# Layer 0's token mixing as three fp32r products of split operands in place of one float32 product

## Chip, cores and metric

The kernel runs on one core of a Trainium2 chip. The metric is the device time of one execution in microseconds (us). In the profile, PE is TensorE's matmul, PEld its weight load, DVE is VectorE, ACT is ScalarE, POOL is GpSimd and SP is SyncE, which issues most DMAs. A line such as L1054 is line 1054 of the kernel before.

## The reference

The program is a two-layer trunk over 256 latent and 256 context tokens of width 2048. Each layer projects the normalised tokens to nine groups of columns, which feed three branches (a: a gated MLP that mixes tokens, b: attention, c: a Fourier mixing), and then projects back. What matters here is branch a:

```python
def chunk_gmlp(u, v, g_sgu, w_s, b_s):
    bsz, t, _ = v.shape
    nc = t // CHUNK
    vn = rmsnorm(v, g_sgu).reshape(bsz, nc, CHUNK, A_HEADS, A_DIM)
    mixed = jnp.einsum('hpq,bcqhd->bcphd', w_s, vn) + b_s.T[None, None, :, :, None]
    return u * mixed.reshape(bsz, t, A_WIDTH)

y_a = chunk_gmlp(jax.nn.gelu(a_u), jax.nn.gelu(a_v), g_sgu, w_s, b_s) * jax.nn.silu(a_g)
```

For each of four heads, every chunk of 128 tokens is multiplied by a 128x128 matrix over its tokens. Layer 0 has four chunks (two latent, two context), layer 1 works on the two latent ones alone.

## The kernel before

Nearly all large products are made in the type fp32r, to which a float32 value is cast with some loss. Each operand is held as a high part (the value cast to fp32r) and a low part (the value minus the high part), and a product is the sum of three: high x high, high x low, low x high. The helper `mm3` (L591 to L594) issues these three matmuls into one accumulator. In layer 0 nearly all of PE's work is of this kind. Branch a's mixing is an exception: a plain float32 matmul, `PE.matmul(ps[...], vt[t][...], ws[:, h], ...)` at L1054.

Weights arrive by the class `Stream` in pieces of 128 x 1024. `load` asks for a piece by DMA into one of three `raw` buffers; `emitting` then casts it on ACT (L560, the high part `whi`) and subtracts on DVE (L562, the low part `wlo`). Pieces are used in a fixed order, and `fetch` emits them up to three pieces ahead of the one that PE uses. Layer 0's opening takes 14 pieces (for av, the columns of v, and for the first three column groups of u), then follow two pieces each for au3 (the last group of u) and for the four groups cx0 to cx3 of the Fourier branch, and so on.

PE's instructions run in the order in which they are written. That order interleaves the column groups (`tunit`, 16 steps k of one `mm3` each) with the pieces of other branches, which are generators that a small clock, `Later`, resumes: each `yield` names how many microseconds of PE work are to pass before the next step, and `tick` advances that clock. From the end of layer 0's opening on, DVE, ACT and SP are not ordered by hand: a scheduler places their instructions by priority, which is the order in which they were emitted, as their inputs become ready in its own reckoning. `low(n)` gives instructions a later priority. Their order on the chip is then fixed.

`branch_a` (L1038 to L1061) is the first such generator behind the opening. Its first step, emitted before au3's products, applies GELU to u (L1042) and to the four chunks `vt` of v (L1044), sums squares (L1046), forms the reciprocal root with POOL's power (L617 to L623), and scales each chunk in place on DVE (L1049). It then yields 11 us of PE work. Each later step is one head: the float32 products of its chunks (L1054), then DVE's scale and bias (L1056), and the product with u (L1060). `fourier_mats` (L1071) comes soon behind it, with `split_into` (L608), which casts on ACT (L609) and subtracts on DVE (L610). In the background `mod_dve` (L310) sums the modulation of later stages on DVE (L321, L323).

Buffers have names (tags), and a tile that is claimed under a tag waits for the release of the one before. `new_yo(k)` claims the output buffer of 16 column groups, two of them in each of `yy0` to `yy7`. At the opening the same tags hold the inputs x, and `yy2`, `yy3` a piece of weights. At L1002 to L1004, when the opening is through, all 16 are claimed. Entries 0 to 3 hold branch a's u (`ytmp`), 12 to 15 the Fourier outputs, 4 to 11 attention.

Of the kernel before, what the change touches and what calls it, by code (L numbers as in the profile page):

```python
# [7 lines left out]
F32 = mybir.dt.float32  # L8
F32R = mybir.dt.float32r
BF16 = mybir.dt.bfloat16  # L10
AF = mybir.ActivationFunctionType
ALU = mybir.AluOpType

P = 128
# [52 lines left out]
def trunk_kernel(ctx: ExitStack, tc: tile.TileContext, xT, xhalf, cT, wss, wsl, wmod, win, wout0, wout1, const, vec, rows,  # L67
                 wmat, bs, sink, out):
    nc = tc.nc
    V, A, G, PE, DMA = nc.vector, nc.scalar, nc.gpsimd, nc.tensor, nc.sync  # L70
# [6 lines left out]
    def sb(shape, dt, tag, bufs=1):  # L77
        cnt[0] += 1
        return pool.tile(shape, dt, tag=tag, bufs=bufs, name=f"{tag}_{cnt[0]}")

    def w2k(shape, dt=F32):
        return sb(shape, dt, "w2k", W2K)
# [5 lines left out]
    def ms_ps(name="ms"):  # L88
        cnt[0] += 1
        return psum.tile([P, 512], F32, tag="ms", bufs=2, name=f"ps_{name}_{cnt[0]}")  # L90
# [18 lines left out]
    def new_yo(j):  # L109
        if j % 2 == 0:  # L110
            t = sb([P, 2, T], F32, f"yy{j // 2}")
            yo[j], yo[j + 1] = t[:, 0], t[:, 1]
        return yo[j]
# [44 lines left out]
    def vc(l, name):  # L158
        o, w = VOFF[name]
        return vecs[:, l, o:o + w]  # L160
# [252 lines left out]
    LOWC = 60  # L413
    LOWP = 60, 0
    YT = 3.0
    GATES = {2: 0, 14: 1}, {14: 2}, {12: 3}, {}
    YG = 6.5
    MODEND = 53.0, 45.0
# [172 lines left out]
    def mm3(ps, st, mv, start, stop):  # L591
        PE.matmul(ps, st[0], mv[0], start=start, stop=False)  # L592
        PE.matmul(ps, st[0], mv[1], start=False, stop=False)  # L593
        PE.matmul(ps, st[1], mv[0], start=False, stop=stop)  # L594

    def part(w, c):

        def of(t):
            if not isinstance(t, list):
                return t[:, c]  # L600
            n = t[0].shape[-1]
            return t[c.start // n][:, c.start % n:c.start % n + c.stop - c.start]

        return of(w[0]), of(w[1])
# [3 lines left out]
    def split_into(hi, lo, src):  # L608
        A.copy(hi, src)  # L609
        V.tensor_tensor(out=lo, in0=src, in1=hi.bitcast(F32), op=ALU.subtract)  # L610
        return hi, lo

    def split_of(src, tag):
        n = src.shape[-1]
        return split_into(sb([P, n], F32R, tag + "h"), sb([P, n], F32R, tag + "l"), src)


    def rstd_cols(sums, n, dim):
        t = sb([P, 4], F32, "rs_a", 2)
        V.tensor_scalar(out=t[:, :n], in0=sums, scalar1=1.0 / dim, scalar2=EPS, op0=ALU.mult, op1=ALU.add)  # L620
        r = sb([P, 4], F32, "rs_b", 2)
        G.tensor_tensor(out=r[:, :n], in0=t[:, :n], in1=mhalf[:, :n], op=ALU.pow)  # L622
        return r  # L623
# [28 lines left out]
    def h_of(l, k, sl):  # L652

        if l == 0:
            return hh[k][:, sl], hl[k][:, sl]
        s, a = sl.start // S, sl.start % S
        t, b = (hh, hl)[s][k], a + sl.stop - sl.start
        return t[:, a:b], t[:, S + a:S + b]
# [75 lines left out]
    def tunit(n, sl=None):  # L734

        sl = slice(0, n) if sl is None else sl
        ps = mm_ps("t")
        for k in range(KT):
            if k % 8 == 0:
                w = W.next()  # L740
            c = slice((k % 8) * P, (k % 8 + 1) * P)
            mm3(ps[:, sl], part(w, c), (hh[k][:, sl], hl[k][:, sl]), k == 0, k == KT - 1)
            later.tick(PASS * n)
        return ps
# [6 lines left out]
    def joined(ps):  # L751

        t = sb([P, S], F32, "join", 2)
        A.copy(t, ps[:, S:T])
        V.tensor_tensor(out=t, in0=t, in1=ps[:, 0:S], op=ALU.add)
        return t

    def tunit1(streams):

        pss = [mm_ps("t") for _ in streams]  # L760
        for k in range(KT):
            if k % 8 == 0:
                w = W.next()
            for s, ps in zip(streams, pss):
                mm2(ps, part(w, slice((k % 8) * P, (k % 8 + 1) * P)), (hh, hl)[s][k], k)
                later.tick(PASS * S)
        return [joined(ps) for ps in pss]
# [12 lines left out]
    def layer(l):  # L780
        last = l == 1
        n = S if last else T
        nt = n // P
# [217 lines left out]
            start_au(k0 + nk - 1)  # L1001
        if l == 0:  # L1002
            for k in range(KT):
                new_yo(k)  # L1004

            DMA.dma_start(cst[:, NFIRST - P:], const[:, NFIRST:NKEEP])
            with low(LOWC):
                for name in ("m0", "ct", "nst"):
                    o, w = COFF[name]
                    raw = w2k([P, w])  # L1010
                    DMA.dma_start(raw, const[:, o:o + w])
                    if w == P:
                        split[name] = sb([P, 2, P], BF16, f"{name}r")
                        raw0 = raw
                        A.copy(split[name][:, 0], raw)
                    else:
                        split[name] = split_of(raw, f"{name}r")

        ws = sb([P, 4, P], F32, "ws")
# [18 lines left out]
        def branch_a():  # L1038
            vt = [w2k([P, 512]) for _ in range(nt)]
            ss = sb([P, 4], F32, "ss")  # L1040
            for j in range(len(au)):
                A.activation(ytmp(j), joined(au[j]) if last else au[j], AF.Gelu_apprx_tanh)  # L1042
            for t in range(nt):
                A.activation(vt[t], av[t], AF.Gelu_apprx_tanh)  # L1044
            for t in range(nt):
                A.activation(av[t], vt[t], AF.Square, accum_out=ss[:, t:t + 1])  # L1046
            r = rstd_cols(ss[:, 0:nt], nt, 512)
            for t in range(nt):
                V.tensor_scalar(out=vt[t], in0=vt[t], scalar1=r[:, t:t + 1], scalar2=None, op0=ALU.mult)  # L1049
            yield 11.0 if l == 0 else 7.0  # L1050
            for h in range(4):
                ps = ms_ps("mix")
                for t in range(nt):
                    PE.matmul(ps[:, t * P:(t + 1) * P], vt[t][:, h * P:(h + 1) * P], ws[:, h], start=True, stop=True)  # L1054
                m = w2k([P, nt, P])
                V.scalar_tensor_tensor(out=m, in0=ps[:, 0:n].rearrange("p (t q) -> p t q", q=P),  # L1056
                                       scalar=vc(l, "gsgu")[:, h:h + 1],
                                       in1=bsb[:, h].unsqueeze(1).to_broadcast([P, nt, P]),
                                       op0=ALU.mult, op1=ALU.add)
                V.tensor_tensor(out=ytmp(h), in0=ytmp(h), in1=m.rearrange("p t q -> p (t q)"), op=ALU.mult)  # L1060
                yield (4.0 if h == 1 else 2.0) if l == 0 else (7.0 if h == 1 else 2.0)  # L1061


# [145 lines left out]
        if l == 0:  # L1209
            later.add(turn_mask(), 1.5)  # L1210
        later.add(branch_a())
        later.add(fourier_mats(), (3.0, 1.5)[l])
        later.tick(0.0)
        state["phase"] = f"au{l}"
        for h in range(len(au), 4):
            ps = tunit1([0])[0] if last else tunit(n)
# [3 lines left out]
        for g in range(4):  # L1220
            ps = tunit1([0])[0] if last else tunit(n)
# [3 lines left out]
        for h in range(4):  # L1225
            ps = tunit1([0])[0] if last else tunit(n)
            gate(h, ps)
        state["phase"] = f"cg{l}"
        for g in range(4):
            ps = tunit1([0])[0] if last else tunit(n)  # L1230
# [3 lines left out]
        r = sb([P, 4, S], F32, "mgl")  # L1234
# [9 lines left out]
        for k in range(KT):  # L1244
# [3 lines left out]
            for t in range(4):  # L1248
                hi, lo = h_of(l, k, slice(t * P, (t + 1) * P))
# [5 lines left out]
        for h in range(8):  # L1255
            ps = tunit1([0])[0] if last else tunit(n)
# [3 lines left out]
        for h in range(8):  # L1260
            ps = tunit1([0])[0] if last else tunit(n)
# [67 lines left out]
    def finish():  # L1329
# [3 lines left out]
        def turn():  # L1333

            for j, tag in enumerate(("vv", "mg", "mgl", "kt0 kt1")):
                tag = tag.split()
                tl = [sb([P, 2 // len(tag), 512], F32, t) for t in tag]
                for t in range(2):
                    x1[j, t] = tl[0][:, t] if len(tl) == 1 else tl[t][:, 0]
                    ps = ms_ps("x1")  # L1340
                    for i in range(4):
                        PE.transpose(ps[:, i * P:(i + 1) * P], yo[4 * j + i][:, t * P:(t + 1) * P], ident)
                    A.copy(x1[j, t], ps)
                    yield YT

        later.add(turn(), YT)
        state["phase"] = "out1"
# [49 lines left out]
        for c in range(4):  # L1397
# [3 lines left out]
            for k in range(KT + back):  # L1401
# [10 lines left out]
                later.tick(PASS * 1024)  # L1412
                if k in GATES[c]:
                    later.add(gate1(GATES[c][k]))
            evac(c, 1, pss[1])
# [92 lines left out]
    with tc.manual_schedule(engines={EN.PE}):  # L1508
# [11 lines left out]
        for i in range(KT):  # L1520
            h, j = i // 8, i % 8
            x = xx[2 * (j // 2) + h][:, j % 2 * 2:j % 2 * 2 + 2]
            q = w2k([P, 2, S])
# [9 lines left out]
            for a in range(2):  # L1533
                k = 2 * j + a
                PE.matmul(sq[32 * (k % 4):32 * (k % 4) + 32, h * S:(h + 1) * S], ones[:, 0:32], q[:, a],
                          start=k < 4, stop=k >= KT - 4, tile_position=(0, 32 * (k % 4)))
# [19 lines left out]
        ps = sums  # L1556
# [22 lines left out]
        for s in range(2):  # L1579
            scale_x(1, rb0, s, 2)  # L1580
        state["e0"] = e
        layer(0)
        state["acc"] = out_proj()
        layer(1)
        finish()

# [76 lines left out]
```

## Time and profile before

| what | value |
|---|---|
| median of three timed runs | 1116.06 us (1115.85 to 1116.09) |
| profiled execution, whole time | 1115.65 us |
| profiled execution, span | 1113.9 us |
| granted TensorE clock | 0.999 |
| ACT busy, share of the span | 49% |
| POOL busy, share of the span | 3% |
| mean DMA rate | 212 GB/s |

The span is the profiled part of an execution; the time around it belongs to start and end. Times in rows are microseconds from the start of the span. In a timeline, a row has the start, the length, the engine, the line, the operation, the output and inputs with shape, and the count of merged instructions; in brackets is how long the engine had been idle and what released it. Matmuls overlap in the pipeline, so their recorded lengths add up to more than the time they hold PE; the distance between starts is the better measure. In the answer for one line, three numbers with slashes are the shortest, median and longest duration in ns.

### The profile page before, as it was taken

What the parts mean: (1) busy time and instruction counts of PE and PEld (TensorE: products, weight loads), DVE (VectorE), ACT (ScalarE), POOL (GpSimd) and SP (SyncE); (2) the same over time, 40 slices, a digit from 0 to 9 for tenths busy, and PEclk for the clock granted to TensorE, in tenths of its full rate; (3) what the DMA queues carried; (4) which work ended last, traced back from release to release, by engine and by line L of the source; (5) the groups of instructions that cost most, each with busy time, mean ns of one, the idle gap of its engine ahead of it and who ended that gap; (6) DMA issues with size and microseconds to landing.
All of it is one profiled execution on the core that took longest, in us unless ns stands there. A gap on an engine that the chain in (4) does not pass through costs nothing. (4 is left out here: it accounts for less than half of the span.)

```text
span 1113.9 us, 17364 instructions
## 1 busy us (share of the span) xinstructions
PE 1104.0 (99%) x6450; PEld 926.4 (83%) x6453; DVE 926.4 (83%) x1616; ACT 550.7 (49%) x1049; POOL 33.4 (3%) x43
## 2 busy tenths in 40 slices
PE   8999999999999999999999999999999999999998
PEld 4777888888888888888888888988888888898886
DVE  3677599999988897988998989397889789878974
ACT  4454823322335667632533333256665379867542
POOL 1000000000000000000000000030500000000000
PEclk9999999999999999999999999999999999999999
DMA  9999655577665353465556665376956686556881
GB/s 376 413 414 410 226 191 169 189 226 215 201 190 174 109 161 114 141 196 184 169 190 209 210 218 177 112 184 202 229 172 206 223 288 199 160 175 205 302 265 75
DMA packets 75525, 235.89 MB, mean 212 GB/s; under 512 B 8480, under 2 KB 15024, under 8 KB 75440
## 3 DMA queue, kind: packets, MB, share of 16 engines
q1 hardware_dynamic: 71088, 230.31, 62.3%
q0 software_dynamic: 4064, 3.69, 2.2%
q8 instruction: 50, 0.82, 0.3%
q10 hardware_dynamic: 288, 0.79, 0.2%
q14 instruction: 35, 0.29, 0.1%
HBM read 232.65 MB, written 2.10 MB: 211 GB/s over the span
## 5 line engine op out<-in xcount | busy, mean ns | idle before, releaser
L560 ACT CAST whi<-raw 128x1024 fp32r<-128x1024 f32 (+1 forms) x210 | 216.6, 1035 | 302.3 <-PE ps_t L593 186.0
L592 PE MATMUL ps_t<-hh,whi 128*128 128x512 f32 (+1 forms) x752 | 290.9, 387 | 0.0
L594 PE MATMUL ps_t<-hh,wlo 128*128 128x512 f32 (+1 forms) x752 | 289.8, 385 | 0.0
L593 PE MATMUL ps_t<-hl,whi 128*128 128x512 f32 (+1 forms) x752 | 289.5, 385 | 0.0
L562 DVE TENSOR_TENSOR wlo<-raw,whi 128x1024 fp32r<-128x1024 f32 (+1 forms) x210 | 251.0, 1199 | 40.6 <-ACT whi L560 34.7
L323 DVE SCALAR_TENSOR_TENSOR macc<-mraw,cs,macc 128x512 f32<-128x512 f32 x360 | 251.5, 745 | 12.7 <-DMA mraw<-in_wmod_dram 12.1
L748 PE MATMUL ps_t<-hh,whi 128*128 128x512 f32 x512 | 181.2, 394 | 0.0
L594 PEld LDWEIGHTS ps_t<-hh,wlo 128*128 128x128 f32 x752 | 141.3, 188 | 28.7
L592 PEld LDWEIGHTS ps_t<-hh,whi 128*128 128x128 f32 x752 | 141.4, 188 | 26.5
L593 PEld LDWEIGHTS ps_t<-hl,whi 128*128 128x128 f32 x752 | 141.4, 188 | 26.4
L749 PE MATMUL ps_t<-hh,wlo 128*128 128x256 f32 x512 | 142.2, 278 | 0.0
L748 PEld LDWEIGHTS ps_t<-hh,whi 128*128 128x128 f32 x512 | 96.2, 188 | 19.3
L749 PEld LDWEIGHTS ps_t<-hh,wlo 128*128 128x128 f32 x512 | 96.2, 188 | 0.4
L592 PE MATMUL ps_y<-whi,hh 128*128 128x512 f32 x104 | 41.3, 397 | 0.0
L594 PE MATMUL ps_y<-whi,hh 128*128 128x512 f32 x104 | 40.6, 391 | 0.0
L593 PE MATMUL ps_y<-wlo,hh 128*128 128x512 f32 x104 | 40.6, 390 | 0.0
L609 ACT CAST w2k<-ps_tp 128x512 fp32r<-128x512 f32 x40 | 23.4, 584 | 21.1 <-PE ps_scc L593 13.6
L610 DVE TENSOR_TENSOR w2k<-ps_tp,w2k 128x512 fp32r<-128x512 f32 x40 | 27.4, 685 | 3.0 <-ACT w2k L609 1.9
L622 POOL TENSOR_TENSOR rs_b<-rs_a,mhalf 128x2 f32<-128x2 f32 (+1 forms) x7 | 6.3, 901 | 751.8 <-DVE mx L1438 582.6
L1172 ACT ACTIVATE w2k<-w2k,den 128x512 f32<-128x512 f32 (+1 forms) x48 | 28.0, 646 | 0.7 <-DVE den L1167 0.6
L827 PE MATMUL ps_av<-whi,hh 128*128 128x512 f32 x64 | 24.4, 396 | 0.1
L592 PE MATMUL ps_o<-w2k,vv 128*128 128x256 f32 x80 | 24.4, 305 | 0.0
(493 smaller groups left out, 1821.5 us busy)
## 6 DMA issues: line engine op xcount, KB each, us to landing
raw<-in_win_dram SPq DMA_DIRECT2D x158, 512.0 KB, 4.3
mraw<-in_wmod_dram SPq DMA_DIRECT2D x128, 512.0 KB, 4.5
raw<-in_wout_dram SPq DMA_DIRECT2D x60, 512.0 KB, 4.4
mraw<-in_wsl_dram SPq DMA_DIRECT2D x12, 512.0 KB, 7.2
yy<-in_xhalf_dram SPq DMA_DIRECT2D x7, 512.0 KB, 7.4
mg<-in_wsl_dram SPq DMA_DIRECT2D x7, 512.0 KB, 8.8
mgl<-in_wsl_dram SPq DMA_DIRECT2D x7, 512.0 KB, 9.2
yy<-in_xhalf_dram POOLq DMA_DIRECT2D x28, 128.0 KB, 7.8
```

Source lines behind the costliest of these rows:

```text
L323: V.scalar_tensor_tensor(out=acc[:, s], in0=w[:, kk % 2], scalar=c, in1=acc[:, s], op0=ALU.mult, op1=ALU.add)
L560: A.copy(ph, rc)
L562: self.last = V.tensor_tensor(out=pl, in0=rc, in1=ph.bitcast(F32), op=ALU.subtract)
L592: PE.matmul(ps, st[0], mv[0], start=start, stop=False)
L593: PE.matmul(ps, st[0], mv[1], start=False, stop=False)
L594: PE.matmul(ps, st[1], mv[0], start=False, stop=stop)
L609: A.copy(hi, src)
L610: V.tensor_tensor(out=lo, in0=src, in1=hi.bitcast(F32), op=ALU.subtract)
L748: PE.matmul(ps, w[0], h, start=k == 0, stop=False)
L749: PE.matmul(ps[:, 0:S], w[1], h[:, 0:S], start=False, stop=k == KT - 1)
L827: PE.matmul(ps, st[a], mv[b], start=start and (a, b) == (0, 0), stop=stop and (a, b) == (1, 0))
L1172: A.activation(prob[i][:, b * w:(b + 1) * w], prob[i][:, b * w:(b + 1) * w], AF.Copy, scale=den[:, c:c + 1])
```

## The change

In layer 0 alone, branch a's normalised v is written as a high and a low part, the mixing weights `ws` are split into high and low, and each float32 product becomes an `mm3`. Layer 1 keeps its float32 product.

The high parts go to the buffers `yy2` and `yy3`, the low parts to `yy5` and `yy7`, the split weights to `yy4`. So that these are free, the ten outputs listed in `YLATE` are claimed only after the last head's products. The scaling on DVE now writes the high part in fp32r, and a second DVE instruction for each chunk, `scalar_tensor_tensor`, multiplies again and subtracts the high part to make the low. The split of the weights is one cast on ACT and one subtraction on DVE.

```diff
+    YLATE = 4, 5, 6, 7, 8, 9, 10, 11, 14, 15
...
         if l == 0:
             for k in range(KT):
-                new_yo(k)
+                if k not in YLATE:
+                    new_yo(k)
...
             r = rstd_cols(ss[:, 0:nt], nt, 512)
-            for t in range(nt):
-                V.tensor_scalar(out=vt[t], in0=vt[t], scalar1=r[:, t:t + 1], scalar2=None, op0=ALU.mult)
+            if last:
+                for t in range(nt):
+                    V.tensor_scalar(out=vt[t], in0=vt[t], scalar1=r[:, t:t + 1], scalar2=None, op0=ALU.mult)
+            else:
+                high, lows = ([sb([P, 2, 512], F32R, f"yy{i}") for i in at] for at in ((2, 3), (5, 7)))
+                wsp = sb([P, 2, 512], F32R, "yy4")
+                wsp = split_into(wsp[:, 0], wsp[:, 1], ws.rearrange("p h q -> p (h q)"))
+                halves = [(high[t // 2][:, t % 2], lows[t // 2][:, t % 2]) for t in range(nt)]
+                for t, (hi, lo) in enumerate(halves):
+                    V.tensor_scalar(out=hi, in0=vt[t], scalar1=r[:, t:t + 1], scalar2=None, op0=ALU.mult)
+                    V.scalar_tensor_tensor(out=lo, in0=vt[t], scalar=r[:, t:t + 1], in1=hi.bitcast(F32),
+                                           op0=ALU.mult, op1=ALU.subtract)
             yield 11.0 if l == 0 else 7.0
             for h in range(4):
                 ps = ms_ps("mix")
                 for t in range(nt):
-                    PE.matmul(ps[:, t * P:(t + 1) * P], vt[t][:, h * P:(h + 1) * P], ws[:, h], start=True, stop=True)
+                    hs, dst = slice(h * P, (h + 1) * P), ps[:, t * P:(t + 1) * P]
+                    if last:
+                        PE.matmul(dst, vt[t][:, hs], ws[:, h], start=True, stop=True)
+                    else:
+                        mm3(dst, part(halves[t], hs), part(wsp, hs), True, True)
...
+                if h == 3 and not last:
+                    for k in YLATE:
+                        new_yo(k)
```

## Prediction

> **What bounds the kernel now.** I read the page first, for the engine that is never free, and then the stretch in which the changed lines lie.
>
> ```profile
> span 1113.9 us, 17364 instructions
> PE 1104.0 (99%) x6450; PEld 926.4 (83%) x6453; DVE 926.4 (83%) x1616; ACT 550.7 (49%) x1049; POOL 33.4 (3%) x43
> ```
>
> PE is busy for 99% of the span, but as averages say little of one stage, the table of stretches for 140 to 190 us, which holds all of layer 0's mixing, comes next.
>
> ```profile
> 140.00:190.00 50.00, 49.96 (x258) 42.47 (x256) 48.40 (x79) 15.35 (x29) 0.00 (x0) 1.00 0.59 190
> ```
>
> The columns are length, then PE, PEld, DVE, ACT and POOL, then the granted clock. PE is idle for 0.04 us of 50 and DVE for 1.6. So every added microsecond of PE work lengthens the kernel, and added DVE work is free only if nothing on PE waits for what stands behind it. ACT has 35 us free. The sum therefore needs two terms: PE's own work, and any wait that the longer DVE queue makes.
>
> **PE's term.** The group of line 1054, then PE's timeline and that of its weight loads around the first head:
>
> ```profile
> L1054 PE MATMUL ps_mix<-ws,w2k x48: 271/275/349, 142.6 to 787.7; 128*128 128x128 f32 x48
> ...
> 142.39 0.39 PE L594 MATMUL ps_t<-hh,wlo 128*128 128x512 f32 x1
> 142.62 1.05 PE L1054 MATMUL ps_mix<-ws,w2k 128*128 128x128 f32 x8
> 143.43 0.48 PE L592 MATMUL ps_t<-hh,whi 128*128 128x512 f32 x1
> 143.74 0.39 PE L593 MATMUL ps_t<-hl,whi 128*128 128x512 f32 x1
> 143.97 0.39 PE L594 MATMUL ps_t<-hh,wlo 128*128 128x512 f32 x1
> ```
>
> The code has 16 products in layer 0 and 8 in layer 1; the group has 48 records, so a float32 product is two passes, and a head with its four products is the row "x8". The recorded lengths overlap, so I go by starts: from the first mixing pass (142.62) to the second ordinary product (143.74) are 1.12 us, of which the ordinary product at 143.43 takes one spacing, 0.23 (143.74 to 143.97). The head holds PE for 0.89 us, 0.111 a pass; four heads hold it for 3.56.
>
> The change puts 12 passes in fp32r where these 8 were. The nearest row for one is the Fourier product of 128 columns at line 1098, fp32r on both sides:
>
> ```profile
> 162.65 0.19 PEld L1098 LDWEIGHTS ps_f<-mg,w2k 128*128 128x128 f32 x1
> 162.76 0.19 PEld L592 LDWEIGHTS ps_f<-mg,w2k 128*128 128x128 f32 x1
> 162.87 0.19 PEld L593 LDWEIGHTS ps_f<-mg,w2k 128*128 128x128 f32 x1
> ...
> 162.76 0.22 PE L1098 MATMUL ps_f<-mg,w2k 128*128 128x128 f32 x1
> 162.82 0.33 PE L592 MATMUL ps_f<-mg,w2k 128*128 128x256 f32 x1
> 162.99 0.28 PE L593 MATMUL ps_f<-mg,w2k 128*128 128x256 f32 x1
> 163.11 0.28 PE L594 MATMUL ps_f<-mg,w2k 128*128 128x256 f32 x1
> ```
>
> Its own columns seem to take 0.06 us (162.76 to 162.82), but in these rows weight loads do not start closer than 0.11 apart, and each of the three products of line 592 to 594 loads anew, also where two share a stationary operand. So 0.111 a pass stays, now as the pace of loading: 48 x 0.111 = 5.33, less 3.56, is **+1.77 us**. The ends: 48 x 0.06 = 2.88, a gain of 0.68, if loads hid entirely; 48 x 0.12 = 5.76 (0.12 from 162.99 to 163.11), +2.20. I take 0.111, the row of the same shape and type.
>
> The Trainium skill has a rule by which the change would gain here. The Trainium skill, "FP8 and Floating Point Precision", section TensorE Precision Notes, counts a true float32 product as four passes through the array. By that, three passes in place of four would take a quarter off the 3.56, -0.89. The trace has two records a product, and at their 0.111 us the four passes would have to run two to a record; what decides is then the pace of 12 single passes, which the fp32r row above gives.
>
> **DVE's term.** DVE's timeline before the first head, and ACT's row for a like cast:
>
> ```profile
> 129.56 0.62 ACT L609 CAST vv<-w2k 128x512 fp32r<-128x512 f32 x1
> ...
> 130.55 0.69 DVE L610 TENSOR_TENSOR vv<-w2k,vv 128x512 fp32r<-128x512 f32 x1
> 131.16 0.75 DVE L323 SCALAR_TENSOR_TENSOR macc<-mraw,cs,macc 128x512 f32<-128x512 f32 x1
> 133.78 0.43 DVE L610 TENSOR_TENSOR ctrl<-w2k,ctrh 128x256 fp32r<-128x256 f32 x1 [1.88 <-ACT ctrh L609]
> 135.59 0.75 DVE L323 SCALAR_TENSOR_TENSOR macc<-mraw,cs,macc 128x512 f32<-128x512 f32 x1 [1.39 <-DMA mraw<-in_wmod_dram]
> 136.26 0.41 DVE L610 TENSOR_TENSOR mg<-ps_mg,mg 128x256 fp32r<-128x256 f32 x1
> 136.60 0.16 DVE L620 TENSOR_SCALAR rs_a<-ss 128x4 f32<-128x4 f32 x1
> 136.67 0.42 DVE L610 TENSOR_TENSOR mg<-ps_mg,mg 128x256 fp32r<-128x256 f32 x1
> 137.95 1.68 DVE L1049 TENSOR_SCALAR w2k<-w2k,rs_b 128x512 f32<-128x512 f32 x4 [0.87 <-POOL rs_b L622]
> 139.54 0.75 DVE L610 TENSOR_TENSOR mgl<-ps_mg,mgl 128x256 fp32r<-128x256 f32 x2
> 140.21 0.41 DVE L610 TENSOR_TENSOR nstrl<-w2k,nstrh 128x256 fp32r<-128x256 f32 x1
> 140.54 3.48 DVE L562 TENSOR_TENSOR wlo<-raw,whi 128x1024 fp32r<-128x1024 f32 x3
> 143.95 2.07 DVE L323 SCALAR_TENSOR_TENSOR macc<-mraw,cs,macc 128x512 f32<-128x512 f32 x3
> ```
>
> Two things are to be read here. First, prices as spacings: the four scalings fill 1.6 us (137.95 to 139.54), 0.40 each; three operations of the form that the lows will have fill 2.07 with the last 0.75 long, so they start (2.07 - 0.75)/2 = 0.66 apart. Four lows add 4 x 0.66 = 2.64 us. The highs are the old scalings with fp32r as output; no row has that, so each costs between 0.40 and the 0.66 of a low: 0 to 1.04 us in all. I take 0, since in other rows (130.55 against 131.16) the fp32r output costs no more than float32. The Trainium skill, "VectorE: DVE Perf Modes", section What auto-detection actually checks, gives the double rate to a one-source operation with source and destination in SBUF, which the highs keep; the 0.40 agrees with the double rate.
>
> Second, what stands behind. The weights come in pieces of 1024 columns, split into high and low in the order of use. Up to 130 us the splits were:
>
> ```profile
> L562 DVE TENSOR_TENSOR wlo<-raw,whi x18: 680/1216/1226, 21.5 to 127.6; 128x1024 fp32r<-128x1024 f32 x10, 128x512 fp32r<-128x512 f32 x8
> L562 DVE TENSOR_TENSOR hh<-raw,hh x1: 684/684/684, 40.9 to 40.9; 128x512 fp32r<-128x512 f32 x1
> L562 DVE TENSOR_TENSOR hl<-raw,hl x1: 693/693/693, 45.1 to 45.1; 128x512 fp32r<-128x512 f32 x1
> L562 DVE TENSOR_TENSOR yy<-raw,yy x1: 1227/1227/1227, 81.2 to 81.2; 128x1024 fp32r<-128x1024 f32 x1
> ```
>
> That is 10 + 4 + 1 + 1 = 16 pieces: 14 for the joint opening of the layer and 2 for au3. The row at 140.54 is thus pieces 17 to 19, and piece 17 is cx0's first. It is done at 140.54 + 1.22 = 141.76 (three start (3.48 - 1.22)/2 = 1.13 apart). cx0's first product with a low weight is the one at 142.39 above, and its load, queued ahead of the first mixing head, is this:
>
> ```profile
> 142.17 0.19 PEld L594 LDWEIGHTS ps_t<-hh,wlo 128*128 128x128 f32 x1
> ...
> 189.44 0.67 DVE L610 TENSOR_TENSOR w2k<-w2k,w2k 128x512 fp32r<-128x512 f32 x1
> ...
> 190.16 0.19 PEld L1098 LDWEIGHTS ps_f<-mgl,w2k 128*128 128x128 f32 x1 [0.52 <-DVE w2k L610]
> ```
>
> So the cover is 142.17 - 141.76 = 0.41 us. The lows come ahead of this split: in the code they stand in branch a's first step, emitted before au3's products, as the scalings do that run ahead of it now. Piece 17 is then ready at 141.76 + 2.64 = 144.40; a load follows its releaser by 0.05 (189.44 + 0.67 to 190.16) and runs its product 0.11 later: 144.56 in place of 142.39. **A wait of 2.17 us.** Queued behind it on PE, which keeps its order, are the mixing heads and all the rest.
>
> What hides the others stands in three more rows:
>
> ```profile
> 116.44 0.33 SPq L1020 DMA_DIRECT2D ws<-in_wmat_dram  x1
> ...
> L1060 DVE TENSOR_TENSOR yy<-yy,w2k x4: 681/681/683, 147.7 to 159.5; 128x512 f32<-128x512 f32 x4
> ...
> L1108 ACT ACTIVATE yy<-ps_z,vecs x4: 685/690/691, 175.0 to 216.0; 128x512 f32<-128x512 f32 x4
> ```
>
> The split of the mixing weights costs ACT 0.62 and DVE 0.61 (130.55 to 131.16). The weights are asked for at 116.44, so it fits in DVE's idle 1.88 or 1.39 us ahead of 136.60; without that cover the wait grows by 0.61. The highs and lows end at 137.95 + 4 x 1.06 = 142.19, ahead of the first head. Pieces 18 and 19 follow 1.13 apart; piece 18, ready at 142.89 now, is wanted after eight k-steps of 3 x 0.23 and two heads, at 141.94 + 5.5 + 1.8 = 149.2: 6 us of cover, so the wait comes once. The five buffers claimed late are first written by Fourier outputs at 175 us or later, or by attention, and the last use of a head's product starts at 159.5; claiming is no instruction and moves no DMA. Loads into raw buffers, freed by the splits, come 2.6 us later into the same 6 us. The stationary and moving sides of layer 1 are untouched.
>
> The sum: 1.77 + 2.17 = 3.94. The profiled execution took 1115.65 (span 1113.9 and 1.75 around it), so 1119.6; the median, 1116.06, lies 0.41 above it, so 1120.0.
>
> **The rivals.** (a) *Not slower: the split of piece 17 is placed ahead of the lows.* It decides as soon as no more than 0.41 us of new DVE work stands before it. For it: DVE's order is made by priority and readiness, and a cast that is ready early may let the split in. Against: nstrl, mgl and the scalings all precede it now. The lows would end at 142.19 + 1.13 = 143.32, in time for the last of the four chunks, wanted 0.111 x 9 after 142.62. Only PE's term is left: 1117.8. (b) *Cheaper passes, as the rule of four passes would have it:* 2.17 - 0.89 gives 1117.3. Against: the 0.11 between loads. (c) *The full bounds on DVE:* highs at 0.66 and the weights' split uncovered, 1.04 + 0.61 more: 1121.7. (d) *Faster:* four of the seven w2k buffers are freed earlier, after the lows and not after the last head. It would have to remove over 6 us of PE idleness to outweigh the sum, and PE is idle for 0.04 us in this stretch.
>
> **How the numbers follow.** About 0.2%, 2.2 us, is what a measurement of this kernel can tell from no change. Forecast 0.62, (a) 0.17, (b) 0.05, (c) 0.12, (d) 0.04. Slower by over 0.2% (above 1118.3) are the forecast and (c): 0.74; within it (a) and (b): 0.22; faster 0.04. The range reaches from just under (a) to just over (c): 1117.5 to 1121.9. The forecast and (c) alone lie in 1118.8 to 1121.9.
>
> **What would show it.** Right: layer 0's 32 mixing records become 48, under the helper's three lines, a head of 12 passes holds PE for 1.33 us, and there is a wait of some 2 us on cx0's first low weight, with DVE's split of line 562 as releaser. Wrong in PE's term: a head under 0.9 us. Wrong in the wait: no PE idleness between 142 and 150 us, with the split ahead of the lows. Wrong altogether: a span no longer than now.

## The result and the profile after

The changed kernel takes 1124.27 us (median of 6 runs, 1122.91 to 1125.56), against 1115.95 for the kernel before on the same chip. The ratio is 1.0073, with a 95% interval of 1.0063 to 1.0083. The forecast was 1120.0 with a range up to 1121.9: slower was right, but the loss is 8.3 us and not 4. The profiled execution took 1124.87.

From L416 on all line numbers grow: the cast is L561 now, the split of the pieces L563, the three matmuls of `mm3` L593 to L595, `split_into` L610 and L611, the highs L1059, the lows L1060, DVE's two steps behind a head L1072 and L1076, the first Fourier additions L1108, the Fourier products L1116 and L1117 (before: L1089, L1097, L1098).

The head of the page after, and then the same stretch of 50 us that held the change before (columns as there: length, PE, PEld, DVE, ACT, POOL, granted clock):

```profile
span 1123.1 us, 17407 instructions
PE 1108.6 (99%) x6469; PEld 929.2 (83%) x6469; DVE 930.1 (83%) x1621; ACT 550.2 (49%) x1050; POOL 33.7 (3%) x43
```

```profile
140.00:190.00 50.00, 45.47 (x228) 38.16 (x227) 48.99 (x80) 11.90 (x21) 0.00 (x0) 0.97 0.52 169
```

PE's busy time grew by 4.6 us and the span by 9.2. In the stretch PE is idle for 4.53 us, where it had been idle for 0.04, and the granted clock is below 1.00. So the loss has three parts: more PE work, idle time, and a slower clock. PE's waits between 100 and 400 us, after, name the idle part (waiting line, releaser, us, times, longest):

```profile
PE ps_t L595 <- DVE wlo L563: 2.3, 1, 2.3
PE ps_f L1116 <- ACT w2k L610: 1.4, 1, 1.4
PE ps_f L1117 <- DVE w2k L611: 0.8, 1, 0.8
```

The first was forecast. The other two, at the first Fourier product, were not. There the first releaser is ACT, but its cast had been waiting for DVE's Fourier additions:

```profile
170.04 0.62 ACT L610 CAST w2k<-w2k 128x512 fp32r<-128x512 f32 x1 [7.03 <-DVE w2k L1108]
```

The following table sets each matmul of after beside the same matmul of before and says where the distance between their starts grows (worked out from the two traces; a head is measured at the products behind it):

| place, time in before | growth, us | forecast |
|---|---|---|
| start of the kernel, and the Fourier matrices (133.7) | 0.28 + 0.20 | 0 |
| cx0's first low weight, up to the first mixing pass (142.6) | 2.54 | 2.17 |
| first head and the products behind it (142.6 to 145.6) | 2.05 | 0.44 |
| heads 2, 3, 4 | 0.47 + 0.47 + 0.48 | 3 x 0.44 |
| first Fourier product (162.6) | 2.79 | 0 |
| second Fourier group (190.2), where before waited | -0.47 | 0 |
| all behind it, most of it at 759 | 0.41 | 0 |
| sum | 9.2 | 3.94 |

**The first low weight.** PE's timeline after, around it and the first head; and one later head:

```profile
145.30 0.50 PE L595 MATMUL ps_t<-hh,wlo 128*128 128x512 f32 x1 [2.27 <-DVE wlo L563]
145.63 0.22 PE L593 MATMUL ps_mix<-yy,yy 128*128 128x128 f32 x1
...
146.03 0.27 PE L594 MATMUL ps_mix<-yy,yy 128*128 128x128 f32 x1
146.14 0.37 PE L595 MATMUL ps_mix<-yy,yy 128*128 128x128 f32 x1
146.31 0.41 PE L593 MATMUL ps_mix<-yy,yy 128*128 128x128 f32 x1
146.52 0.41 PE L594 MATMUL ps_mix<-yy,yy 128*128 128x128 f32 x1
...
147.59 0.73 PE L593 MATMUL ps_t<-hh,whi 128*128 128x512 f32 x1
148.12 0.63 PE L594 MATMUL ps_t<-hl,whi 128*128 128x512 f32 x1
148.55 0.63 PE L595 MATMUL ps_t<-hh,wlo 128*128 128x512 f32 x1
...
151.33 0.22 PE L593 MATMUL ps_mix<-yy,yy 128*128 128x128 f32 x1
...
152.51 0.28 PE L595 MATMUL ps_mix<-yy,yy 128*128 128x128 f32 x1
152.62 0.45 PE L593 MATMUL ps_t<-hh,whi 128*128 128x512 f32 x1
```

The later head takes 152.62 - 151.33 = 1.29 us to the next ordinary product; by the same measure the head of before takes 0.81 (142.62 to 143.43). But in the first head the passes start 0.11 apart only up to 146.14, and then 0.21 apart (146.31 to 146.52), and the 512-column products behind it 0.43 apart (148.12 to 148.55) and not 0.23. The table of stretches after says why (the clock is the third number from the end):

```profile
146.20:149.60 3.40, 3.40 (x13) 3.01 (x13) 3.40 (x5) 0.76 (x1) 0.00 (x0) 0.50 0.83 247
```

Just behind the wait PE had half its clock for 3.4 us. That is at most 1.7 us lost, and 2.05 - 0.47 = 1.58 is what the table above has left for it.

**DVE.** Its timeline after, in the stretch that the prediction read:

```profile
133.94 0.69 DVE L611 TENSOR_TENSOR yy<-ws,yy 128x512 fp32r<-128x512 f32 x1 [1.73 <-ACT yy L610]
...
137.07 0.16 DVE L621 TENSOR_SCALAR rs_a<-ss 128x4 f32<-128x4 f32 x1
137.14 0.75 DVE L323 SCALAR_TENSOR_TENSOR macc<-mraw,cs,macc 128x512 f32<-128x512 f32 x1
138.79 0.88 DVE L1059 TENSOR_SCALAR yy<-w2k,rs_b 128x512 fp32r<-128x512 f32 x2 [0.90 <-POOL rs_b L623]
139.59 1.41 DVE L1060 SCALAR_TENSOR_TENSOR yy<-w2k,rs_b,yy 128x512 fp32r<-128x512 f32 x2
...
144.03 1.22 DVE L563 TENSOR_TENSOR wlo<-raw,whi 128x1024 fp32r<-128x1024 f32 x1
...
158.03 3.40 DVE L323 SCALAR_TENSOR_TENSOR macc<-mraw,cs,macc 128x512 f32<-128x512 f32 x5
161.34 0.75 DVE L1072 SCALAR_TENSOR_TENSOR w2k<-ps_mix,vecs,bsb 128x512 f32<-128x512 f32 x1
...
168.61 0.41 DVE L1108 TENSOR_TENSOR w2k<-ps_t,w2k 128x254 f32<-128x254 f32 x1
...
171.20 0.68 DVE L611 TENSOR_TENSOR w2k<-w2k,w2k 128x512 fp32r<-128x512 f32 x1
```

Up to 144 us it is what was forecast: the weights' split fills idle time, two highs of 0.48 fill 0.88, so they are 0.40 apart, two lows of 0.75 fill 1.41, 0.66 apart, and the piece's split stands behind all four. New is what comes between the heads: five background sums in one row, ahead of the step that waits for a head's product (161.34). Grouped by line, from the row statistics (`rs_a`) to the first Fourier addition, before (136.7 to 159.2 us) and after (137.0 to 168.6 us):

```profile
L323 DVE SCALAR_TENSOR_TENSOR macc<-mraw,cs,macc 128x512 f32<-128x512 f32 x11 | 7.9, 743 | 0.0
```

```profile
L323 DVE SCALAR_TENSOR_TENSOR macc<-mraw,cs,macc 128x512 f32<-128x512 f32 x19 | 13.4, 746 | 0.8 <-DMA mraw<-in_wmod_dram 0.8
```

The diff does not touch the sums, yet 19 and not 11 stand ahead of the Fourier branch now. The scheduler that fixes DVE's order before the run has moved them forward.

How tight that place was can be read in DVE's timeline of before, with the row of the load at 162.65 that the prediction shows:

```profile
159.21 0.41 DVE L1089 TENSOR_TENSOR w2k<-ps_t,w2k 128x254 f32<-128x254 f32 x1
...
161.80 0.68 DVE L610 TENSOR_TENSOR w2k<-w2k,w2k 128x512 fp32r<-128x512 f32 x1
```

The first Fourier product's operand was ready at 161.80 + 0.68 = 162.48, its load started at 162.65; less the 0.05 that a load follows its releaser, the cover was 0.12 us. DVE had been busy since 137.95 with no gap above 0.04 us. So PE's next wait there is what DVE comes later, less what PE comes later, less 0.12.

### The profile page after: what moved, and what is told of

Read it like the earlier page. It is cut to its first block, busy times and chain, and to the rows that moved or that the text cites. A ratio compares the mean times of both kernels' runs of the same rounds, so it can differ in the third digit from the quotient of the medians.

```text
span 1123.1 us, 17407 instructions
## 1 busy us (share of the span) xinstructions
PE 1108.6 (99%) x6469; PEld 929.2 (83%) x6469; DVE 930.1 (83%) x1621; ACT 550.2 (49%) x1050; POOL 33.7 (3%) x43
## 5 line engine op out<-in xcount | busy, mean ns | idle before, releaser
L561 ACT CAST whi<-raw 128x1024 fp32r<-128x1024 f32 (+1 forms) x210 | 216.5, 1035 | 311.1 <-PE ps_t L594 199.7
L595 PE MATMUL ps_t<-hh,wlo 128*128 128x512 f32 (+1 forms) x752 | 289.9, 386 | 2.3 <-DVE wlo L563 2.3
L593 PE MATMUL ps_t<-hh,whi 128*128 128x512 f32 (+1 forms) x752 | 291.1, 387 | 0.0
L563 DVE TENSOR_TENSOR wlo<-raw,whi 128x1024 fp32r<-128x1024 f32 (+1 forms) x210 | 251.0, 1199 | 47.0 <-ACT whi L561 40.0
L595 PEld LDWEIGHTS ps_t<-hh,wlo 128*128 128x128 f32 x752 | 141.5, 188 | 31.8 <-DVE wlo L563 2.7
L593 PEld LDWEIGHTS ps_t<-hh,whi 128*128 128x128 f32 x752 | 141.6, 188 | 26.4
L593 PE MATMUL ps_y<-whi,hh 128*128 128x512 f32 x104 | 41.3, 397 | 0.0
L595 PE MATMUL ps_y<-whi,hh 128*128 128x512 f32 x104 | 40.6, 390 | 0.0
L610 ACT CAST w2k<-ps_tp 128x512 fp32r<-128x512 f32 x40 | 23.4, 584 | 21.1 <-PE ps_scc L594 13.6
L611 DVE TENSOR_TENSOR w2k<-ps_tp,w2k 128x512 fp32r<-128x512 f32 x40 | 27.4, 684 | 3.0 <-ACT w2k L610 1.9
L593 PE MATMUL ps_o<-w2k,vv 128*128 128x256 f32 x80 | 24.3, 304 | 0.0
```

Of the source, the lines that this page charges most:

```text
L561: A.copy(ph, rc)
L563: self.last = V.tensor_tensor(out=pl, in0=rc, in1=ph.bitcast(F32), op=ALU.subtract)
```

## The experiments

Theory A holds the lows responsible for both waits: they lengthen DVE's queue, and without them, or with them elsewhere, the waits go. Theory B: the wait at the Fourier product comes from the order of DVE's background sums, which the three products in the program text move forward, lows or none. For the clock there are two theories as well: idle time halves it, or the dense short passes of a head do. Ratios are to the kernel before on the same chip.

**split_first**: the split of cx0's first piece between highs and lows.

```diff
                 for t, (hi, lo) in enumerate(halves):
                     V.tensor_scalar(out=hi, in0=vt[t], scalar1=r[:, t:t + 1], scalar2=None, op0=ALU.mult)
+                W.emit()
+                for t, (hi, lo) in enumerate(halves):
                     V.scalar_tensor_tensor(out=lo, ...)
```

> The changed kernel, with cx0's first weight piece cast and split between the highs and the lows, so that DVE makes its low part before the lows. Theory A (separate losses): the wait on the low piece (2.5 us) and the slow clock behind it (1.65 us) both go and the wait at the first Fourier product stays as it is: 1124.3 - 4.1 = 1120.2 us. Theory B (DVE's queue sets the Fourier product's time): 19 background sums still stand ahead of the Fourier branch's first additions, where 11 stood before, so the first Fourier product can start only some 1.2 us earlier than 170.7, and the Fourier wait grows by what the first wait loses: about 1123 us, with an idle PE of 4 us or more at the Fourier product.

Measured: 1126.41 us, ratio 1.0098 (1.0083 to 1.0113). PE's waits between 130 and 360 us:

```profile
PE ps_f L1118 <- ACT w2k L610: 4.6, 1, 4.6
PE ps_mg L593 <- ACT m0r L1036: 0.9, 1, 0.9
PE ps_f L1119 <- DVE w2k L611: 0.6, 1, 0.6
```

The wait on the low weight is gone, and the kernel is slower. PE, no longer held up there, meets DVE at the Fourier product (19 sums again) and waits for 5.2 us, with the clock at 0.50 from 168.8 to 175.6 us. B, and more than B had reckoned. The wait at `ps_mg`, 0.9 us, stands in all three kernels with the split moved and in no other.

**three_no_low**: the three products from the high parts alone; the low parts of values and weights are left out of the computation, and so are the instructions that make them.

> The three fp32r products per head and chunk, all made from the high parts; the low parts of v and of the mixing weights are left out (the high stands in their place), so DVE has none of the new work. Theory A: no wait left, only PE's term: 1116.0 + 1.8 + 0.3 = 1118 us. Theory B: the order still follows from the longer reckoned products (22 background sums ahead of the Fourier additions), no wait on the low piece, but one of 4 us or more at the first Fourier product: 1122 to 1123 us.

Measured: 1126.13, ratio 1.0095 (1.008 to 1.011), with no low part made at all:

```profile
PE ps_f L1115 <- ACT w2k L610: 5.6, 1, 5.6
PE ps_f L1116 <- DVE w2k L611: 0.6, 1, 0.6
```

22 sums stand ahead of the Fourier branch. A falls for this wait: without lows it is the longest of all. The run one_pass, below, differs from this one in a single line, one product in place of the three, and has 13 sums there.

**lows_one_f32**: the lows are made but read by nothing, and the product is the float32 one of before.

> Highs, lows and the weights' split are made as in the changed kernel, but the mixing is the one float32 product of before, from an unrounded high; the lows are written and not read. Theory A: everything but PE's term stays: 1124.3 - 1.8 = 1122.5 us. Theory B: 9 background sums ahead of the Fourier additions, so no wait there; what stays is the wait on the low piece, 2.3 us, and the slow clock behind it, 1.65 us: about 1120.2 us.

Measured: 1118.01, ratio 1.0025 (1.0015 to 1.0035); 9 sums, and one wait:

```profile
PE ps_t L595 <- DVE wlo L563: 1.7, 1, 1.7
```

Together with the run before this takes the change apart: the lows on DVE make the wait on the low weight and nothing else, the three products in the program make the longer row of sums: this kernel and the changed one differ in little but the product, and have 9 and 19. The clock stayed at 1.00 in the profiled execution, which is why B's 1120.2, with 1.65 us in it for the clock, was not reached, and why the next kernel had nothing to show.

**lows_f32_fill**: the same with ten products of zeros ahead of the waiting product.

> As the kernel with lows and one float32 product, with ten bf16 products of zeros (512 columns, about 2.2 us) put on PE just ahead of the product that waits for the low piece. If the idleness of the wait halves the clock, the granted clock stays at 1.00 behind it and 1.65 us are saved: about 1118.5 us, for the same start of the waiting product. If something else halves it (the dense run of short products, a weight-load limit), it is 0.50 here too and the time stays at 1120.2 us.

Measured: 1119.18, ratio 1.0031 (1.0018 to 1.0043). Inconclusive on the clock, which was not halved without them either.

Three runs then shift the sums with the table `RATE`, which says how densely steps of `mod_dve`, four sums each, are asked for in each stage.

**split_few_mods** and **few_mods**: fewer early, more later, with and without the split moved; **few_mods_fill** has the ten products too. The three expectations follow in this order, and so do the times.

```diff
-    RATE = dict(au0=2, cx0=2.2, ag0=2.2, cg0=2.2, k0=2, ...
+    RATE = dict(au0=0, cx0=0.6, ag0=3.2, cg0=3.2, k0=2.4, ...
```

> The changed kernel with the split of cx0's first piece placed between the highs and the lows, and with lower numbers for the opening in the table of rates, so that 11 background sums, as before the change, and not 19 stand on DVE between branch a's statistics and the first Fourier addition. Theory B (the wait at the first Fourier product comes from the longer DVE queue of background sums): neither wait is left, and the time is that of before, 1115.4, and the passes, 1.8, and up to 1.1 for a wait on ps_mg: 1117.2 to 1118.8. Theory A (the wait at the Fourier product belongs to the changed products or their lows, whatever the order of the sums): it stays at 4 to 5 us, and the time stays near 1126.

> The changed kernel, with only the rates lowered: 11 background sums, and the lows ahead of cx0's first split, as in the change. Theory B: the wait on the first low weight stays at 2.3 us, that at the Fourier product is gone; with the passes 1.8, and 1.6 for a clock halved after the wait, 1121.2; without the halved clock 1119.6. Theory A: as the change, 1124.3.

> The kernel with lowered rates, and in it ten products of zeros, 512 columns each, put on PE ahead of the product that waits for the first low weight, so that PE is not idle there. If the 2.3 us of idleness halve the granted clock, the clock stays at 1.00 from 146 to 150 us and the time is 1.6 below that of the kernel with lowered rates alone, about 1119.6. If the clock is halved for another reason (the load of the short passes that follow), it is halved here too and the two times agree, near 1121.2.

Measured: 1124.58, ratio 1.0076 (1.0062 to 1.009); 1125.72, ratio 1.0087 (1.0072 to 1.0103); 1125.63, ratio 1.0089 (1.0075 to 1.0102). All three times miss what B expected, though its step is there: the wait at the Fourier product is gone in each. A new one stands at the first scores of attention, in split_few_mods and in few_mods (its rows second):

```profile
PE ps_sc L593 <- ACT w2k L610: 4.3, 1, 4.3
```

```profile
PE ps_sc L593 <- ACT w2k L610: 3.6, 1, 3.6
PE ps_t L595 <- DVE wlo L563: 1.7, 1, 1.7
```

The stretches of split_few_mods before and at that point (columns: length, PE, PEld, DVE):

```profile
170.00:190.00 20.00, 20.00 (x105) 17.18 (x104) 10.51 (x22) 7.53 (x16) 0.00 (x0) 1.00 0.33 107
...
345.00:360.00 15.00, 10.66 (x44) 8.53 (x43) 14.90 (x26) 5.83 (x10) 0.00 (x0) 0.89 0.43 141
```

I had cut too deep: DVE was half idle from 170 to 190 us and then had the sums to make up, up to attention; the smaller cut of the next kernels leaves no wait at these scores. Of the clock, few_mods and few_mods_fill show in their stretches that it stayed at 1.00 with the products (146 to 150 us) and was 0.62 without. In the two traces this puts PE 1.1 us ahead up to attention, but the medians of four executions each agree, so the timing does not show it.

**split_paced** and **paced**: the pace is 0 only through au0 and cx0's first group, and that of before afterwards; **paced_fill** is paced with the ten products.

```diff
-    RATE = dict(au0=2, cx0=2.2, ...
+    RATE = dict(au0=0, cx0=2.2, ...
...
         for g in range(4):
+            if l == 0:
+                state["phase"] = "au0" if g < 1 else "cx0"
```

> The changed kernel with cx0's first split placed between the highs and the lows, and with the background sums left out of the pace through au0 and the first group of cx0 alone (rate 0 there, the rates of before afterwards): 13 sums stand ahead of the first Fourier addition in DVE's order (the change: 19; before: 11), and 144 ahead of attention's keys (before: 160). If what the sums take from DVE is all that is left of the loss (theory B), neither the Fourier product nor the first scores of attention wait: 1115.5 + 1.8 for the passes + 0.3 to 1.1 for ps_mg = 1117.6 to 1118.4. If the first scores wait for sums that come later, whatever the pace, it stays above 1121.

Measured: 1121.73, ratio 1.0055 (1.0041 to 1.0069). The wait at the scores is gone, but the time is above what was expected, because 0.8 us are left at the Fourier product and 0.5 at the first head, and because two waits that before has not, 0.5 and 0.4 us, stand in layer 1's attention (at 927.7 and 948.9 us; paced, paced_fill and one_paced have them too):

```profile
PE ps_mg L593 <- ACT m0r L1036: 0.9, 1, 0.9
PE ps_f L1119 <- DVE w2k L611: 0.8, 1, 0.8
PE ps_mix L593 <- DVE mgl L611: 0.5, 1, 0.5
```

> The change as it is (lows ahead of cx0's first split), with the pace of background sums set to 0 through au0 and the first group of cx0 alone: 13 sums ahead of the first Fourier addition instead of 19. Reckoning by DVE's order: DVE comes to the Fourier product 2.64 (lows) + 2 x 0.66 (sums) = 3.96 us later than before, PE 1.8 (passes) + 2.3 (first low weight) + 0 to 1.6 (clock) = 4.1 to 5.7 later, so no wait there. The time is 1115.5 + 4.1 to 5.7 + up to 0.5 at ps_mg = 1119.6 to 1121.7. If the wait at the Fourier product is there with any order, it stays at 1124.

> The same pace, and ten products of zeros, 512 columns each, ahead of the product that waits for the first low weight. If idleness halves the clock and the loss of it costs 1.6 us, the clock is 1.00 from 142 to 150 us and the time is 1.6 below that of the same pace without them, unless DVE then becomes the later one at the Fourier product: PE comes there 1.8 + 2.6 = 4.4 later than before, DVE 3.96, so a cover of 0.5 us is left. If the clock is halved for another reason the two times agree.

Measured: paced 1122.15, ratio 1.0057 (1.0045 to 1.007); paced_fill 1121.18, ratio 1.0048 (1.0034 to 1.0061). Waits between 130 and 360 us, of paced and of paced_fill:

```profile
PE ps_t L595 <- DVE wlo L563: 2.4, 1, 2.4
```

```profile
PE ps_t L748 <- DVE wlo L563: 0.2, 1, 0.2
PE ps_f L1124 <- DVE w2k L611: 0.2, 1, 0.2
```

paced is the change with nothing but the pace altered, and its only wait in this stretch is the forecast one: the wait at the Fourier product belongs to the order. Its time is 0.45 us above the expected range, which was reckoned from 1115.5; the kernel before took 1116.1 beside it. The two side by side then settle the clock, in paced and in paced_fill:

```profile
146.90:150.20 3.30, 3.30 (x10) 2.61 (x9) 3.30 (x5) 1.04 (x1) 0.00 (x0) 0.51 0.90 274
```

```profile
146.90:150.20 3.30, 3.30 (x19) 2.78 (x18) 3.25 (x5) 1.05 (x1) 0.00 (x0) 1.00 0.81 273
```

The same heads with the same 12 passes follow in both; with PE kept busy through the wait the clock stays at 1.00. Idle time halves it, not the passes. The other executions agree: the mean clock is 0.997 or 0.998 in all five of paced, and 0.999 or 1.000 in all five of paced_fill. Behind the last head paced_fill is 6.39 - 4.81 = 1.58 us ahead, as expected; 0.43 of that it gives back at the Fourier product, where PE is now the earlier one, and the spans differ by 1.0 (1120.4 and 1119.4). The intervals of the two ratios overlap, so the profile, not the timing, carries the price of the clock.

**one_pass** and **one_paced**: one fp32r product of the high parts alone, with the pace of before and with that of paced; the low parts are left out of the computation.

```diff
-                        mm3(dst, part(halves[t], hs), part(wsp, hs), True, True)
+                        PE.matmul(dst, halves[t][0][:, hs], wsp[0][:, hs], start=True, stop=True)
```

> Layer 0's mixing by one fp32r product of the high parts instead of three; the low parts of values and weights are left out of the computation. 16 passes in place of before's 32. If a short fp32r pass costs 0.111 us, as one of the two records of a float32 product does, PE saves 1.78 us: 1113.7. If a float32 product costs four passes of the fp32r kind, it saves more: 16 passes in 3.56 us less three quarters, 1112.8. With 13 background sums ahead of the first Fourier addition no wait there is expected; if one comes, it is added.

> The single fp32r product of high parts (low parts left out) with the same pace: 11 background sums ahead of the first Fourier addition instead of 13. If the gain of 1.8 us of passes was given back only to the wait for DVE's sums there (theory B), the time is 1113.7 to 1114.5. If PE, being earlier, waits for DVE there with any number of sums, it stays at 1116.

Measured: 1116.38, ratio 1.0006 (0.9997 to 1.0014), and 1116.22, ratio 1.0006 (0.9997 to 1.0015): not told from the kernel before. PE saves what the passes cost, 0.46 or 0.47 us a head for 4 passes fewer (4 x 0.111 = 0.44), 1.86 in all; and gives it back at the first Fourier products. The waits of one_pass between 130 and 360 us:

```profile
PE ps_f L1116 <- DVE w2k L611: 1.4, 3, 0.6
PE ps_f L1115 <- ACT w2k L610: 0.5, 1, 0.5
```

With 11 sums, as before the change, one_paced still waits there for 0.8 us. I had expected it to keep the gain. DVE is only 0.33 us earlier than before and PE 1.68, and the cover was 0.12.

All of this is one account. "DVE later" is the start of the subtraction that makes the first Fourier product's low part, less 161.80; "PE later" is how far PE's matmuls stand behind those of before at the last product ahead of it (162.42 in before); the reckoned wait is the first less the second less 0.12. The growth is measured from there to the first product of L592 behind it (162.82).

| kernel | sums ahead | DVE later | PE later | reckoned | growth at the Fourier product |
|---|---|---|---|---|---|
| after | 19 | 9.40 | 6.49 | 2.79 | 2.79 |
| split_first | 19 | 9.60 | 3.48 | 6.00 | 6.11, clock halved in it |
| three_no_low | 22 | 9.27 | 2.17 | 6.98 | 7.09, clock halved in it |
| lows_one_f32 | 9 | 1.91 | 2.27 | none | none |
| lows_f32_fill | 12 | 2.94 | 2.20 | 0.62 | 0.62 |
| few_mods | 11 | 3.98 | 5.68 | none | none |
| few_mods_fill | 11 | 3.76 | 4.53 | none | none |
| split_few_mods | 11 | 2.68 | 3.15 | none | none |
| split_paced | 13 | 4.96 | 3.74 | 1.10 | 1.11 |
| paced | 13 | 6.52 | 6.39 | 0.01 | 0.01 |
| paced_fill | 13 | 5.37 | 4.81 | 0.44 | 0.43 |
| one_pass | 13 | 0.04 | -1.80 | 1.72 | 1.72 |
| one_paced | 11 | -0.33 | -1.68 | 1.23 | 1.23 |

For after, DVE's 9.40 are: four lows 2.64; seven more sums behind the release of `rs_b` 7 x 0.66 = 4.62, the eighth standing ahead of it; the later release 0.84 (138.79 against 137.95); the wait of a sum for its data 0.81; one more subtraction of `split_into` behind the release, 0.33. That makes 9.24.

No version of the change beats the kernel before. The best of them is paced_fill at 1.0048. Of the 5.5 us that its span is longer, 2.7 lie at the first low weight, 1.9 are the passes and 0.43 the Fourier product; the rest are small steps either way.

## Why the forecast was too low

**PE's term was right.** Forecast +1.77 for 48 passes in place of 32 at 0.111. Heads 2 to 4 grew by 0.47, 0.47 and 0.48, where 0.44 was forecast, and the mixing records after are 16 under each of the three lines:

```profile
L593 PE MATMUL ps_mix<-yy,yy x16: 220/274/415, 145.6 to 162.6; 128*128 128x128 f32 x16
L594 PE MATMUL ps_mix<-yy,yy x16: 272/276/415, 145.7 to 162.7; 128*128 128x128 f32 x16
L595 PE MATMUL ps_mix<-yy,yy x16: 274/276/415, 145.8 to 162.8; 128*128 128x128 f32 x16
```

The rival by the rule of four passes, (b), has fallen: it wanted a head of 12 passes to be shorter than one of 8 float32 records, and one_pass shows that a record costs what a single fp32r pass costs. By (b) a head's 0.89 us would be 16 passes, and one_pass, with 4 of them left, would have saved three quarters, 0.67 us a head; 0.46 or 0.47 were saved. What fell is the price, not the count: two passes of the 0.06 us that the columns of the Fourier product seemed to take would also fit into one record of 0.111, and no run tells.

**DVE's prices and the first wait were right.** Highs at 0.40, lows at 0.66, the weights' split hidden in idle time, and a wait of 2.27 where 2.17 was forecast, at the product that was named; the four lows stand ahead of the piece's split, and lows_one_f32, with the lows alone, has the wait too.

**"So the wait comes once" failed.** The step looked for what stands behind the lows among the pieces of weights, where pieces 18 and 19 indeed had cover, and did not follow DVE's queue on to the next product that needs it, 20 us later, where the cover was 0.12 us. With DVE's order as before the step would still have held: DVE would have come 2.64 us later and PE 3.94; paced, with 13 sums, bears this out. But it took that order as fixed. It changed: 19 sums in place of 11, and a second wait, 2.79 us by the table. That the three products move the sums is shown by three_no_low, one_pass and lows_one_f32; that the wait follows the sums by paced, few_mods and their like. Why the scheduler brings them forward, no run shows; that it reckons the three products as longer than they are, and so sees DVE free, would fit, and is left open.

**A term was missing: the clock behind a wait.** The 2.27 us of idle time cost another 1.58, shown by paced and paced_fill. The prediction put nothing down for it. With these two terms, 2.79 + 1.58, the forecast's 3.94 becomes 8.31; the rest of the 9.2 is 0.37 at the first wait, 0.12 in the heads and steps of 0.4 to 0.5 either way.

**Rival (a) failed too, and in its sign.** With the split ahead of the lows it gave 1117.8; split_first takes 1126.41. The wait it removes had been hiding a longer one. (c), at 1121.7, came nearest to 1124.27, but by luck: the highs cost 0.40 and the weights' split was covered. (d) did not occur. What was read right, that DVE is idle for 1.6 us of 50 in this stretch, was used only for the lows' own delay; it says that DVE is the second limit all along it.

## What to carry to other kernels

Where a second engine is as full as the bottleneck, find each point at which the two meet and its cover, and follow an added delay through all of them: a wait that is removed or a pass that is saved ahead of the tightest is only waited out there. Where a scheduler places the background work, an edit to one engine's products can reorder another engine's queue: count what stands ahead of each meeting point before and after. And price an idle stretch of PE by its length and by the clock behind it.

## What the runs showed of the hardware

The clock: after 2.27 us of idle time (after) it was 0.50 for 3.4 us. Within a run, all recorded changes of the clock lie whole multiples of 3.413 us apart: in after they are at 9.64, 146.18 (40 of them later) and 149.59, in few_mods at 145.63, 149.04, 357.26 (61 of them later) and 360.67. So the idle time can be counted within each of these stretches. Where the clock was halved, the stretch that ended there held 2.27 us of it in after, 1.68 in paced (of a wait of 2.43) and 1.66 in few_mods. The two idle pieces of 1.42 and 0.83 at the Fourier product of after fall into two stretches, with 0.78 and 1.48, and left it at 1.00. In lows_one_f32 one stretch (142.52 to 145.94, counted from the change at 9.40) held 1.72 and the clock stayed at 1.00; two of its nine executions have a mean clock of 0.997 and 0.998, the others 0.999 or 1.000. So the border lies near half a stretch, about 1.7 us, and no run here tells what decides at it.

The Trainium skill, "TensorE: Matmul & The Clock Gate", section What's actually happening, has two ratios, 4/8 and 8/8, and a free-running window of about 3.4 us; the 0.50, the 3.4 us and the whole multiples agree. The same page of the Trainium skill, section Why this matters for your kernels, warns of gaps of over about 3 us; here 1.66 and 2.27 us were enough.

POOL beside DVE: from the start of `rs_a` to the highs there are 1.35 us in before, where no sum stands between (and 1.36 or 1.37 in the three kernels with the split moved), and 1.72 in after, with a sum at 137.14 in between (1.71 to 1.73 in the nine other kernels with one there). What makes the difference was not tried.
